# Moving work from GpSimd and the residual of one output group in a streaming mixer layer

## The chip, the cores and the metric

The kernel runs on one core of one Trainium2 chip. The metric is the device time of one execution in microseconds: the median of the runs shown. The profile is of one further execution of the same program.

Engines are named as in the profile: PE is TensorE's matmul, PEld its weight load, DVE is VectorE, ACT is ScalarE, POOL is GpSimd, SP is SyncE, which here only issues DMAs.

## The reference

One mixer layer is applied to 1024 rows of a new stream and 64 rows of a running one, with 2048 features each:

```
h = RMSNorm(x);  z = h @ w_in                      # 2048 x 7296, 57 blocks of 128 columns
A: vn = LayerNorm(gelu(v));  f = tril(W_s) @ vn + b   # per 128-row chunk and head group
   out_a = gelu(u) * f * silu(g_a)
B: zs mixed with its previous row (token shift) -> r, k, v, and two low-rank inputs
   decay = exp(-exp(-softplus(-d) - 0.5)), a = sigmoid(...)
   kk = k * k_k / |k * k_k|;  k = k * (1 + (a - 1) * k_a)
   S = S * decay - (S kk) (kk a)^T + v k^T;  y = S r     # 16 heads of 64, over time
   y = GroupNorm(y) + (sum r k r_k) v;  out_b = y * silu(g_b)
o = [out_a ; out_b] @ w_out;  y = RMSNorm(x + o)
```

Outputs are the normalised rows of both streams, the final states S, the last shifted rows and the vn of the running stream.

## The kernel before, in words

**Precision and tiling.** Large products are made of three float16 matmuls each (high and low halves of both operands, line list `PASSES`). The normalised input lies transposed in SBUF as two float16 copies in one large tile (`bigt`, 16 blocks of 1088 columns each). The input projection walks over 57 weight blocks; each block takes three groups of 364, 364 and 360 columns with 48 matmuls, into one of two PSUM banks called `mp`. A weight block is loaded as float32 (`raw`), scaled and split into its two halves by ACT and DVE (`w`).

**Pairs.** Part B treats the 16 heads as 8 pairs. The generator `front(q)` (line 825) prepares pair q: low-rank products, decay and its running products, the normalised kk, the new k, and whole-tile products of 128x1088 that end as the packed tiles AR and KB. The generator `wkv(q)` (line 928) takes chunks of 64 rows in groups of up to four: two matmuls per chunk and head fill a PSUM bank (`bigp`) with four 64x64 blocks per chunk (the Gram blocks). Those are copied to the tile MK (named `wk` in the profile, as AR, KB and others share it) and multiplied by a strictly lower or a lower triangular mask. A triangular inverse on DVE follows (60 small products and transposes), then a chain of 17 chunk steps in which PE makes a 128x128 product (`yps`), DVE adds it to the values, PE makes the next (`smp`), and DVE updates the state S. `post(q)` normalises, gates and writes the result to HBM.

**Output.** The output weights come in 16 jobs: two halves of the 16 feature blocks times 8 groups of 256 columns. `out_first` (line 1355) does group 0 of the first half; it does the first six feature blocks of four row blocks and then the last two, as these come late. Then `out_group` does the others. Each group's accumulator is a slice of `bigt` (`acc_view`), whose place is free once the input projection has read it. It is loaded with x, the residual, by `acc_load` (line 1410), and `out_add` (line 1348) adds a scaled PSUM bank to it on DVE. Loads for groups 1 to 7 go out on POOL's queue, that for group 0 on ACT's.

**Order.** The order on every engine is written out by a planner in Python at build time. It keeps a clock for each engine (`self.clk`), charges each instruction an estimated cost (`act`, `stt`, `tt`, `mm`), and walks through PE's main work, the projection. Between matmuls `poll()` lets side generators go on whose due time (the value they yielded) has come, and only if DVE's clock is not further ahead of PE's than the generator's backlog. A generator that waits for a flag or for room in PSUM yields until it is there. Engines run their instructions strictly in that order; only semaphores hold them up on the chip.

**Places that the change touches.** In the profile nearly all instructions stand under a helper's line: 186 is `act`, 194 `stt`, 203 and 201 `tt`, 245 `mm`, 253 `dma`. Line 201 is the branch of `tt` that cuts a whole-tile product on POOL into two instructions; the planner charges both together 200 ns and 2.2 ns a column. On DVE it charges 150 ns and one column per 0.96 GHz cycle.

Of the kernel before, what the change touches and what calls it, by code (L numbers as in the profile page):

```python
# [10 lines left out]
AF = mybir.ActivationFunctionType  # L11
ALU = mybir.AluOpType
# [4 lines left out]
NP, NS = 1024, 64  # L17
# [27 lines left out]
class Builder:  # L45
# [779 lines left out]
    def front(self, q):  # L825
        nc = self.nc
# [4 lines left out]
        for j in range(2):  # L831
            f = self.dma(nc.sync, lw[:, j], self.a["lora"][j, :, q * 128:(q + 1) * 128], 1 << 16)
# [3 lines left out]
        for j in range(2):  # L836
            f = self.act(self.lwh[:, j, 0], lw[:, j], AF.Copy, scale=self.lws[j][0])
        yield f - 200
        for j in range(2):
            f = self.stt(self.lwh[:, j, 1], lw[:, j], self.lws[j][0], self.lwh[:, j, 0], ALU.mult, ALU.subtract, dep=f)  # L840
        yield max(f, fh)
        c = yield from self.galloc(RES)
        C = self.U(c)
# [3 lines left out]
        f = self.fin(DV, 2800)  # L847
        fh = self.dma(nc.sync, hw, self.hw_d[:, NT:2 * NT], 1 << 18)
        yield f
        p = yield from self.galloc(RES)  # L850
        PX = self.u[p][:, 0:NCH * 65].rearrange("p (c t) -> p c t", t=65)
        nc.gpsimd.memset(PX[:, :, 0:1], 1.0)
        v3 = lambda x: x.rearrange("p (c t) -> p c t", t=64)
# [5 lines left out]
        aa = self.U(ai)  # L859
# [3 lines left out]
        k = yield from self.z_load(32 + q, RES)  # L863
        K = self.U(k)
        sq = yield from self.galloc(RES)
        SQ = self.U(sq)
        yield self.act(SQ, K, AF.Square, scale=self.vcol(V_KK, q))
        for hs in self.head_sums(SQ):
            if isinstance(hs, tuple):
                f = self.act(hs[0], hs[1], AF.Ln)  # L870
# [4 lines left out]
        yield self.stt(SQ, SQ, 1e12, K, ALU.min, ALU.mult)  # L875
        t = yield from self.galloc(RES)
        T = self.U(t)
        yield self.tt(T, SQ, aa, ALU.mult, eng=nc.gpsimd)
        yield self.ts(aa, aa, self.vcol(V_KA, q), self.oka[:, q:q + 1], ALU.mult, ALU.add)
        yield self.tt(K, K, aa, ALU.mult, eng=nc.gpsimd)  # L880
        self.free(ai)
        yield self.tt(T, T, C, ALU.mult, eng=nc.gpsimd)
        yield self.tt(v3(SQ), v3(SQ), PX[:, :, 0:64], ALU.mult, eng=nc.gpsimd)
        if q:
            yield from self.wait(("c16", q - 1))
        for hp in HP:
# [1 line left out]
        r = yield from self.z_load(24 + q, RES)  # L888
        R = self.U(r)
        RP = PX[:, :, 1:65]  # L890
        yield self.tt(RP, v3(R), RP, ALU.mult, eng=nc.gpsimd)
        yield self.stt(R, R, self.vcol(V_RK, q), K, ALU.mult, ALU.mult)
        yield self.tt(K, K, C, ALU.mult, eng=nc.gpsimd)
        self.free(c)
        yield from self.wait("f")
        v = P["v"] = yield from self.z_load(40 + q, RES)
        V = self.U(v)
        nk = self.nkk[:, q:q + 1]
        for part, (c0, c1) in enumerate(PARTS):
# [6 lines left out]
            f = self.copy(self.AR[:, cs, 1, :], RP[:, cs])  # L906
            for i in range(2):
                ci = slice(c0 + i, c1, 2)
                f = self.act(self.KB[:, ci, 1 - i, :], v3(T)[:, ci], AF.Copy, scale=nk)
                f = max(f, self.copy(self.KB[:, ci, i, :], v3(K)[:, ci]))  # L910
# [5 lines left out]
        for hs in self.head_sums(R, V):  # L916
            if isinstance(hs, tuple):
                f = self.tt(hs[2], hs[1], hs[2], ALU.mult)
# [4 lines left out]
        f = self.dma(nc.sync, self.bv_d[q], V, 1 << 19)  # L923
# [4 lines left out]
    def wkv(self, q):  # L928
        nc = self.nc
        P = self.pr[q]  # L930
        AR, KB, MK, KBt, VS = self.AR, self.KB, self.MK, self.KBt, self.VS
        v3 = self.U(P["v"]).rearrange("p (c t) -> p c t", t=64)
# [3 lines left out]
        mv = MK.rearrange("p (r c) g k -> p c r g k", r=2)  # L936
# [69 lines left out]
        for part, (c0, c1) in enumerate(PARTS):  # L1006
            yield from self.wait(("ark", q, part))
            self.add(vtr(part), backlog=1e9)
            for c in range(c0, c1, 4):
                m = min(4, c1 - c)  # L1010
                yield from self.room("big", "big")
                pts = [self.bigt() for _ in range(2)]
                for r in range(m):
                    for h in range(2):
                        self.mm(pts[h][:, r * 128:(r + 1) * 128], KB[HP[h], c + r].rearrange("p s t -> p (s t)"),
                                AR[HP[h], c + r].rearrange("p s t -> p (s t)"))
                for h in range(2):
                    f = self.act(mv[:, c:c + m, :, h, :],
                                 pts[h][:, 0:m * 128].rearrange("p (c r k) -> p c r k", r=2, k=64), AF.Copy)
                for r in range(2):  # L1020
                    v = MK[:, 17 * r + c:17 * r + c + m]
                    f2 = self.tt(v, v, self.mask[:, r * 64:r * 64 + 64].unsqueeze(1).unsqueeze(1)
                                 .to_broadcast([128, m, 2, 64]), ALU.mult, eng=nc.gpsimd, dep=f)
                    fm = fm if r else f2
                a0, a1 = max(c, 1), min(c + m, 16)
                if a0 < a1:
                    self.tt(af[:, a0:a1], af[:, a0:a1], pc[:, a0 - 1:a1 - 1].unsqueeze(2)
                            .to_broadcast([128, a1 - a0, 128]), ALU.mult, eng=nc.gpsimd)
                yield f - 300
            self.add(ktr(part), backlog=1e9)  # L1030
# [18 lines left out]
        for i in range(1, 31):  # L1049
            n = 31 - i  # L1050
# [3 lines left out]
            f = self.tt(X[:, i + 1:32, 0:i], X[:, i + 1:32, 0:i], pv, ALU.add)  # L1054
# [5 lines left out]
        f = self.vtr(ent(PT), X, rate=0.58)  # L1060
        yield f
        PG = PR.rearrange("p (c g t) -> p c g t", g=2, t=32)
        for p0, par, n in SIDE:
            self.act(MA[p0:p0 + 32, par:NCH:2, :, 0:32], PG[p0:p0 + 32, 0:n], AF.Copy)
            f = self.copy(MA[p0 + 32:p0 + 64, par:NCH:2, :, 32:64], PG[p0 + 32:p0 + 64, 0:n])
# [34 lines left out]
        pts = [self.bigt() for _ in range(2)]  # L1100
# [246 lines left out]

    def out_add(self, g, st, t, nt, ps):
        a = self.acc_view(g)[:, t:t + nt, :]
        while ("acc", g) not in self.flags:  # L1350
            self.spin()
        return self.stt(a, ps[:, 0:nt * 256].rearrange("p (t n) -> p t n", n=256), self.sc[st][:, 4:5], a,
                        ALU.mult, ALU.add)

    def out_first(self, st):
        w = self.wb[st]
        self.out_scale(0, st)
        self.add(self.acc_load())
        for t0 in (0, 4):
            ps = [self.ps_main.tile([128, 512], F32, tag="m", name="mp") for _ in range(2)]  # L1360
            for kts in (range(6), range(6, 8)):
                for p in range(2):
                    for r in range(2):
                        self.out_mm(0, ps[p], r, t0 + 2 * p + r, w, kts, kts[0] == 0 and r == 0, r == 1)
                    if kts[0]:
                        self.out_add(0, st, t0 + 2 * p, 2, ps[p])
        self.out_sample(0, w, self.mixT[0], self.sc[st][:, 4:5])

    def out_part(self, half, g, st, t, nt):
# [39 lines left out]

    def acc_load(self):  # L1410
        nc = self.nc
        self.accs = self.big[:, 16384:17408].rearrange("p (j t) -> p j t", t=64)
        for g in range(8):
            if g == 1:
                yield from self.wait(("mixT", 0))
            if g >= 4:
                yield from self.wait("moved")
            self.dma(nc.gpsimd if g else nc.scalar, self.acc_view(g),
                     self.a["x"][0:NP, g * 256:(g + 1) * 256].rearrange("(t p) n -> p t n", p=128))
            if g == 0:  # L1420
                nc.gpsimd.dma_start(self.accs, self.a["xts"])
            self.flags.add(("acc", g))
            yield self.now + 10000

    def fg_load(self):
        while len(self.ufree) < 5:
# [218 lines left out]
```

## Time and profile before

| | |
|---|---|
| median of 3 runs | 1983.4 us (1980.28 to 1984.43) |
| profiled execution | 1978.55 us, its span 1976.8 us, granted PE clock 0.996 |
| PE busy | 1920.4 us (97%) |
| DVE busy | 1152.3 us (58%) |
| ACT busy | 1027.6 us (52%) |
| POOL busy | 352.5 us (18%) |

The span begins with the first instruction and ends with the last; the execution's time is 1.75 us longer. Busy time is the union of an engine's instructions. PE's matmuls are pipelined, so the durations of single ones overlap and their mean says little; the time of a long row of them, divided by their number, is what one costs. The input projection ends at about 1584 us; the output projection follows, with the last pair's chain laid over its first two groups.

### The profile page before, as it was taken

Reading aid. Unit: us, or ns where it says so; the run is one execution under the profiler, and the core shown is the slowest. Engines: PE = TensorE matmul, PEld = TensorE weight load, DVE = VectorE, ACT = ScalarE, POOL = GpSimd, SP = SyncE. Lnnn points to the kernel's source line nnn. Section 1 sums busy time; section 2 is a strip of 40 time slices with the busy share of each in tenths; the row PEclk is TensorE's granted clock in tenths of the full one; section 3 lists DMA queues with packets and bytes.
Section 4 is the critical chain, followed back from the end, with each engine's and each line's share of the span. In section 5 each row is a group of like instructions: output and inputs, shape, how many; then the busy total and the mean of one; then the engine's idle time right before and its main releaser. Section 6 shows DMA issues by size and latency. Waiting matters only on the chain. (4 is left out here: it accounts for less than half of the span.)

```text
span 1976.8 us, 42947 instructions
## 1 busy us (share of the span) xinstructions
PE 1920.4 (97%) x18429; PEld 1391.8 (70%) x18429; DVE 1152.3 (58%) x2557; ACT 1027.6 (52%) x1862; POOL 352.5 (18%) x360
## 2 busy tenths in 40 slices
PE   6999999999999999999999999999999989999998
PEld 5966666666666666676676666666666678899997
DVE  6574684355565658449559446564753776533444
ACT  7632344467556554755664746646564542422433
POOL 2400000320410340150231042033014311000000
PEclk9999999999999999999999999999999999999999
DMA  6221124213122322313212321221232355312114
GB/s 239 87 76 43 46 80 148 111 54 106 67 81 69 112 87 72 113 57 114 87 72 69 124 101 48 103 99 65 72 112 79 131 174 181 145 62 99 56 44 140
DMA packets 51758, 188.98 MB, mean 96 GB/s; under 512 B 6832, under 2 KB 18624, under 8 KB 41904
## 3 DMA queue, kind: packets, MB, share of 16 engines
q1 hardware_dynamic: 41200, 153.99, 22.3%
q0 software_dynamic: 6880, 22.26, 3.2%
q10 hardware_dynamic: 3488, 9.99, 1.3%
q8 instruction: 145, 2.38, 0.5%
q14 instruction: 45, 0.37, 0.1%
HBM read 140.32 MB, written 45.93 MB: 94 GB/s over the span
## 5 line engine op out<-in xcount | busy, mean ns | idle before, releaser
L245 PE MATMUL mp<-bigt,w 128*128 128x364 f16 (+3 forms) x8496 | 1323.1, 310 | 4.7 <-issue 2.6
L245 PEld LDWEIGHTS <-w 128*128 128x128 f16 x9216 | 815.8, 98 | 410.4 <-issue 3.9
L194 DVE SCALAR_TENSOR_TENSOR w<-raw,sci,w 128x512 f16<-128x512 f32 x276 | 221.7, 827 | 158.6 <-ACT w L186 157.8
L245 PEld LDWEIGHTS <-wk 128*128 128x128 f16 x2304 | 209.6, 98 | 28.5 <-issue 5.2
L186 ACT ACTIVATE w<-raw,sci 128x512 f16<-128x512 f32 x276 | 185.7, 713 | 57.9 <-DVE sci L303 49.1
L245 PE MATMUL mp<-w,wk 128*128 128x256 f16 x1728 | 203.7, 273 | 5.1 <-DVE bigt L194 5.1
L201 POOL TENSOR_TENSOR u<-u,u 128x544 f32<-128x544 f32 (+1 forms) x112 | 156.5, 1424 | 256.5 <-DVE u L194 105.4
L186 ACT ACTIVATE w<-raw 128x2048 bf16<-128x2048 f32 (+1 forms) x70 | 131.8, 1883 | 82.8 <-PE mp L245 82.2
L186 ACT ACTIVATE wk<-bigp 128x512 f32<-128x512 f32 (+6 forms) x248 | 121.0, 512 | 84.9 <-PE bigp L245 55.5
L245 PE MATMUL mp<-w,u 128*128 128x256 f16 x1152 | 141.2, 273 | 0.0
L186 ACT ACTIVATE u<-mp,sc 128x364 f32<-128x364 f32 (+3 forms) x109 | 57.0, 523 | 153.4 <-PE mp L245 152.6
L186 ACT ACT_TABLE_LOAD x91 | 116.8, 1283 | 23.4 <-PE smp L245 7.1
L194 DVE SCALAR_TENSOR_TENSOR bigt<-mp,sc,bigt 128x512 f32<-128x512 f32 (+2 forms) x83 | 54.1, 652 | 127.9 <-PE mp L245 127.5
L186 ACT ACTIVATE u<-yps 64x128 f32<-64x128 f32 x120 | 32.7, 273 | 182.8 <-DVE wk L203 182.1
L245 PEld LDWEIGHTS <-u 128*128 128x128 f16 x1152 | 112.1, 98 | 13.5
L1131 DVE SCALAR_TENSOR_TENSOR S<-S,pc,smp 64x64 f32<-64x64 f32 x240 | 66.8, 278 | 75.3 <-PE smp L245 70.5
L203 POOL TENSOR_TENSOR wk<-wk,mask 128x512 f32<-128x512 f32 (+1 forms) x80 | 83.2, 1059 | 137.8 <-ACT wk L186 137.8
L186 ACT ACTIVATE u<-mp,zs 128x364 f32<-128x364 f32 (+1 forms) x75 | 42.1, 562 | 121.4 <-PE mp L245 121.0
L203 DVE TENSOR_TENSOR u<-u,u 128x108 f32<-128x108 f32 (+15 forms) x248 | 91.4, 368 | 8.3
L203 DVE TENSOR_TENSOR u<-bigp,u 128x512 f32<-128x512 f32 (+3 forms) x72 | 41.5, 579 | 87.4 <-PE smp L245 57.0
L194 DVE SCALAR_TENSOR_TENSOR u<-mp,zs,u 128x363 f32<-128x363 f32 (+1 forms) x100 | 49.5, 495 | 66.8 <-ACT sht L186 35.4
L223 DVE STREAM_TRANSPOSE wk<-u 32x256 f32<-32x256 f32 (+1 forms) x128 | 58.0, 453 | 45.4 <-ACT u L186 43.5
(182 smaller groups left out, 1883.4 us busy)
## 6 DMA issues: line engine op xcount, KB each, us to landing
raw<-w_in SPq DMA_DIRECT2D x54, 1024.0 KB, 5.0
raw<-w_out SPq DMA_DIRECT2D x14, 1024.0 KB, 5.0
z_d<-u SPq DMA_DIRECT2D x24, 544.0 KB, 3.3
u<-z_d SPq DMA_DIRECT2D x24, 544.0 KB, 5.8
mix_d<-u ACTq DMA_DIRECT2D x16, 544.0 KB, 3.0
o_y<-bigt SPq DMA_DIRECT2D x16, 512.0 KB, 4.1
u<-mix_d POOLq DMA_DIRECT2D x15, 544.0 KB, 7.4
wk<-x SPq DMA_DIRECT2D x7, 1024.0 KB, 7.6
```

Of the source, the lines that this page charges most:

```text
L186: self.nc.scalar.activation(out, in_, func, bias=bias, scale=scale, **kw)
L194: self.nc.vector.scalar_tensor_tensor(out, in0, s, in1, op0, op1)
L201: eng.tensor_tensor(out[:, c], a[:, c], b[:, c], op)
L203: (eng or self.nc.vector).tensor_tensor(out, a, b, op)
L223: self.nc.vector.transpose(out, a)
L245: self.nc.tensor.matmul(out, lhsT, rhs, start=start, stop=stop)
L1131: self.nc.vector.scalar_tensor_tensor(Sn[hp, hp], Sc[hp, hp], pc[hp, c - 1:c], pu[hp, hp], ALU.mult, ALU.add)
```

## The change

Three edits go together.

1. The first output group is evicted by ACT as a plain scaled copy into its accumulator. Its share of x is no longer loaded ahead; after the last pair has been written out, it is loaded in two halves on SP's queue into two temporary tiles and added by DVE. The second half's eviction of group 0 waits for a flag, `("res", 0)`, that is set then. The loads of the other groups are issued without the planner's pause behind the first.
2. The Gram blocks are no longer copied by ACT and then masked in place by POOL in two instructions; DVE multiplies the PSUM bank by the mask as it evicts it. The generator yields after each of the two.
3. Six whole-tile products of `front` move from POOL (two instructions each) to DVE (one each).

```diff
@@ front
-        yield self.tt(T, SQ, aa, ALU.mult, eng=nc.gpsimd)
+        yield self.tt(T, SQ, aa, ALU.mult)
...
-        yield self.tt(K, K, aa, ALU.mult, eng=nc.gpsimd)
+        yield self.tt(K, K, aa, ALU.mult)
...
-        yield self.tt(T, T, C, ALU.mult, eng=nc.gpsimd)
-        yield self.tt(v3(SQ), v3(SQ), PX[:, :, 0:64], ALU.mult, eng=nc.gpsimd)
+        yield self.tt(T, T, C, ALU.mult)
+        yield self.tt(v3(SQ), v3(SQ), PX[:, :, 0:64], ALU.mult)
...
-        yield self.tt(RP, v3(R), RP, ALU.mult, eng=nc.gpsimd)
+        yield self.tt(RP, v3(R), RP, ALU.mult)
...
-        yield self.tt(K, K, C, ALU.mult, eng=nc.gpsimd)
+        yield self.tt(K, K, C, ALU.mult)
@@ wkv
                 for h in range(2):
-                    f = self.act(mv[:, c:c + m, :, h, :],
-                                 pts[h][:, 0:m * 128].rearrange("p (c r k) -> p c r k", r=2, k=64), AF.Copy)
-                for r in range(2):
-                    v = MK[:, 17 * r + c:17 * r + c + m]
-                    f2 = self.tt(v, v, self.mask[:, r * 64:r * 64 + 64].unsqueeze(1).unsqueeze(1)
-                                 .to_broadcast([128, m, 2, 64]), ALU.mult, eng=nc.gpsimd, dep=f)
-                    fm = fm if r else f2
+                    f = self.tt(mv[:, c:c + m, :, h, :],
+                                pts[h][:, 0:m * 128].rearrange("p (c r k) -> p c r k", r=2, k=64),
+                                self.mask[:, 0:128].rearrange("p (r k) -> p r k", k=64).unsqueeze(1)
+                                .to_broadcast([128, m, 2, 64]), ALU.mult)
+                    fm = f + 300
+                    yield f - 400
@@ out_add
-        while ("acc", g) not in self.flags:
+        while ("acc" if g else "res", g) not in self.flags:
@@ out_first
-        self.add(self.acc_load())
+        self.accs = self.big[:, 16384:17408].rearrange("p (j t) -> p j t", t=64)
+        self.add(self.acc_load(), backlog=1e9)
...
-                        self.out_add(0, st, t0 + 2 * p, 2, ps[p])
+                        t = t0 + 2 * p
+                        self.act(self.acc_view(0)[:, t:t + 2, :].rearrange("p t n -> p (t n)"), ps[p][:], AF.Copy,
+                                 scale=self.sc[st][:, 4:5])
+        while ("acc", 0) not in self.flags:
+            self.spin()
@@ acc_load
-            self.dma(nc.gpsimd if g else nc.scalar, self.acc_view(g),
-                     self.a["x"][0:NP, g * 256:(g + 1) * 256].rearrange("(t p) n -> p t n", p=128))
-            if g == 0:
+            if g:
+                self.dma(nc.gpsimd, self.acc_view(g), self.x_cols(g))
+            else:
                 nc.gpsimd.dma_start(self.accs, self.a["xts"])
             self.flags.add(("acc", g))
-            yield self.now + 10000
+            yield self.now + 10000 * (g > 0)
+        yield from self.wait(("mix", 15))
+        for h in range(2):
+            i = yield from self.galloc(1)
+            x = self.u[i][:, 0:1024].rearrange("p (t n) -> p t n", n=256)
+            yield self.dma(nc.sync, x, self.x_cols(0)[:, 4 * h:4 * h + 4], 1 << 19)
+            a = self.acc_view(0)[:, 4 * h:4 * h + 4]
+            yield self.tt(a, a, x, ALU.add)
+            self.free(i)
+        self.flags.add(("res", 0))
```

`x_cols(g)` is the slice of x that belongs to group g.

## Rows read from the trace of the kernel before

**Rows 1.** The page: busy us, share of span, instructions of each engine.

```profile
PE 1920.4 (97%) x18429; PEld 1391.8 (70%) x18429; DVE 1152.3 (58%) x2557; ACT 1027.6 (52%) x1862; POOL 352.5 (18%) x360
```

**Rows 2.** Windows, nine stretches from 300 to 1576 us: total length, busy us by engine.

```profile
sum 1276.00, PE 1249.77 PEld 841.11 DVE 754.38 ACT 746.57 POOL 298.90; mean PE 138.86 PEld 93.46 DVE 83.82 ACT 82.95 POOL 33.21
```

**Rows 3.** Timeline of the first output group: start, duration, instruction, [idle before, releaser].

```profile
1590.72 4.09 PE L245 MATMUL mp<-w,u 128*128 128x256 f16 x36
1590.73 0.42 ACTq L253 DMA_DIRECT2D bigt<-x  x1
1591.35 1.93 ACT L186 ACTIVATE w<-raw,sci 128x512 f16<-128x512 f32 x3
1591.89 0.78 DVE L194 SCALAR_TENSOR_TENSOR u<-bigt,pwi,u 128x544 f16<-128x544 f32 x1
...
1599.11 0.71 DVE L194 SCALAR_TENSOR_TENSOR bigt<-mp,sc,bigt 128x512 f32<-128x512 f32 x1
...
1599.87 1.44 PE L245 MATMUL mp<-w,wk 128*128 128x256 f16 x6 [5.06 <-DVE bigt L194]
...
1601.75 0.63 ACT L186 ACTIVATE wk<-u 32x512 f32<-32x512 f32 x1 [8.46 <-DVE u L223]
```

**Rows 4.** PE's timeline, three rows that begin after an idle time.

```profile
504.13 0.49 PE L245 MATMUL smp<-wk 128*128 128x128 f32 x2 [2.18 <-DVE wk L203]
...
1139.34 0.46 PE L245 MATMUL smp<-wk 128*128 128x128 f32 x2 [2.21 <-DVE wk L203]
...
1470.26 0.49 PE L245 MATMUL smp<-wk 128*128 128x128 f32 x2 [0.38 <-DVE wk L203]
```

**Rows 5.** Timelines of POOL and DVE, in a chain's steps and after the last.

```profile
498.70 5.03 POOL L201 TENSOR_TENSOR u<-u,u 128x544 f32<-128x544 f32 x4
499.44 4.33 DVE L211 TENSOR_SCALAR gss<-gss 64x2 f32<-64x2 f32 x1
...
651.96 3.60 POOL L201 TENSOR_TENSOR u<-u,u 128x544 f32<-128x544 f32 x2
652.25 2.13 DVE L203 TENSOR_TENSOR u<-u,gst 128x1024 f32<-128x1024 f32 x1
...
1440.49 0.16 DVE L211 TENSOR_SCALAR gss<-gss 64x2 f32<-64x2 f32 x1
...
1670.89 1.22 DVE L203 TENSOR_TENSOR u<-u,gst 128x1024 f32<-128x1024 f32 x1
```

**Rows 6.** Groups by form: line, engine, operation, shapes, count, busy us, mean ns.

```profile
L201 POOL TENSOR_TENSOR u<-u,u 128x544 f32<-128x544 f32 x80 | 115.1, 1462 | 222.8 <-DVE u L194 105.4 <-issue 59.8 <-DVE u L213 45.2
L203 POOL TENSOR_TENSOR wk<-wk,mask 128x512 f32<-128x512 f32 x64 | 76.2, 1210 | 137.8 <-ACT wk L186 137.8
...
L201 POOL TENSOR_TENSOR u<-u,u 128x576 f32<-128x576 f32 x16 | 21.3, 1330 | 0.0
L201 POOL TENSOR_TENSOR u<-u,u 128x512 f32<-128x512 f32 x16 | 21.2, 1326 | 33.7 <-DMA u<-z_d 33.7
...
L203 DVE TENSOR_TENSOR u<-bigp,u 128x512 f32<-128x512 f32 x32 | 22.0, 690 | 81.7 <-PE smp L245 57.0 <-PE bigp L245 19.0 <-DMA f_d<-u 4.6
...
L203 DVE TENSOR_TENSOR u<-u,u 128x1088 f32<-128x1088 f32 x8 | 11.7, 1459 | 0.1
...
L203 POOL TENSOR_TENSOR wk<-wk,pc 128x512 f32<-128x512 f32 x24 | 26.8, 1117 | 0.0
...
L186 ACT ACTIVATE wk<-bigp 128x512 f32<-128x512 f32 x112 | 62.5, 595 | 67.2 <-PE bigp L245 43.6 <-PE bigp L250 22.5 <-PE smp L245 0.9
```

**Rows 7.** Timelines of ACT and PE: last pair's final pass, group 0's second half.

```profile
1690.54 1.11 ACT L186 ACTIVATE u<-u 128x1088 f32<-128x1088 f32 x1 [7.78 <-DVE u L194]
...
1788.97 4.09 PE L245 MATMUL mp<-w,wk 128*128 128x256 f16 x36
```

**Rows 8.** Windows, two neighbouring stretches: bounds, then length and busy us.

```profile
1150.00:1200.00 50.00, 48.32 (x387) 32.93 (x385) 16.75 (x42) 25.32 (x49) 26.74 (x25) 1.00 0.26 89
1200.00:1250.00 50.00, 50.00 (x446) 32.33 (x444) 44.95 (x103) 24.02 (x43) 3.46 (x5) 1.00 0.21 68
```

In these two rows the columns after the length are the busy times of PE, PEld, DVE, ACT and POOL with their instruction counts, then the granted PE clock, the DMA engines' share and GB/s.

More of the change, by code (lines that the diff above doesn't have):

```diff
@@ L1411, in acc_load @@
         nc = self.nc
-        self.accs = self.big[:, 16384:17408].rearrange("p (j t) -> p j t", t=64)
         for g in range(8):
@@ L1417, in acc_load, with x_cols @@
                 yield from self.wait("moved")
-            self.dma(nc.gpsimd if g else nc.scalar, self.acc_view(g),
-                     self.a["x"][0:NP, g * 256:(g + 1) * 256].rearrange("(t p) n -> p t n", p=128))
-            if g == 0:
+            if g:
+                self.dma(nc.gpsimd, self.acc_view(g), self.x_cols(g))
+            else:
                 nc.gpsimd.dma_start(self.accs, self.a["xts"])
             self.flags.add(("acc", g))
-            yield self.now + 10000
+            yield self.now + 10000 * (g > 0)
[8 more added lines that the diff above has]
+        self.flags.add(("res", 0))
+    def x_cols(self, g):
+        return self.a["x"][0:NP, g * 256:(g + 1) * 256].rearrange("(t p) n -> p t n", p=128)
     def fg_load(self):
```

## The prediction

> **What bounds the kernel now.** I read the busy times of the page first. TensorE (PE) is busy 1920.4 us of a span of 1976.8 us [rows 1], so a change that leaves every matmul as it is, as this one does, can only win back idle time of PE: 56.4 us in all. No more than that is at stake, whatever the other engines save. The start (PE idle while the first rows of x are normalised) and the tail after the last matmul are not touched. The stretch that the change does touch runs from 300 us, where the pairs begin, to the first output group at 1600 us. From 300 to 1576 us PE is busy 1249.77 of 1276.00 us, so 26.2 us are idle [rows 2], and one more gap of 5.06 us follows at 1599.87 us [rows 3].
>
> The next view is PE's timeline, of which I took the rows that carry an idle time in brackets. Two things are to be seen there [rows 4]. Most gaps stand in front of the small float32 matmuls of the state chain (tiles smp and yps) and name VectorE (DVE) as the releaser: DVE is late with the sum or the new state that the next step multiplies. Between 300 and 1576 us I count 23 gaps of 0.38 us or more, 25.1 us together. During 12 of them, the first at 504.13 and the last at 1470.26 us, GpSimd (POOL) was in one of its whole-tile products; these are 11.75 us. The other 11 sum to 13.4 us and have other causes: an early wait for a write to HBM, DVE held up behind a ScalarE (ACT) result (the 2.21 us at 1139.34), and stretches where PE waits for nothing that the profile shows.
>
> The timeline of DVE and POOL side by side says why POOL matters [rows 5]. A DVE TENSOR_SCALAR on 64x2 elements, 0.16 us when POOL is quiet (1440.49), starts at 499.44 and takes 4.33 us: it ends at 503.77, as POOL's row of 5.03 us that began at 498.70 ends at 503.73. The chain's addition stood behind it, and PE lost 2.18 us. In the same way a product of 128x1024 took 2.13 us at 652.25, under POOL's row of 3.60 us from 651.96, and 1.22 us at 1670.89, where POOL did no arithmetic.
>
> **The change part by part.** *First output group.* Today its eviction adds the residual, whose load was issued on ACT's queue at 1590.73 us; DVE evicts at 1599.11 (0.71 us), and PE, which needs the bank for its second four blocks, stands still for 5.06 us until 1599.87 [rows 3]. After the change ACT evicts with a scale and no load is needed. ACT is done with the weight preparation at 1591.35 + 1.93 = 1593.28 us and then waits until 1601.75. One eviction of 128x512 from PSUM costs ACT about 0.60 us [rows 6]. PE's first bank is complete twelve matmuls ahead of the second, 1.4 us at 4.09 us for 36, so it is free when PE comes back: the whole gap goes. What is late next is the eighth tile of the output's left operand, whose last piece DVE finishes at 1591.89 + 0.78 = 1592.67 us, about when PE gets to it. If DVE is a microsecond later there, PE stands for that microsecond. I bound the gain by 3 and 5.3 us and take 5.
>
> The residual of that group comes back at the end of the last pair: two loads on SP's queue, two DVE additions of 128x1024 at 1.22 us [rows 5]. The last pair's ACT pass ends at 1690.54 + 1.11 = 1691.65 us and the group's second half starts on PE at 1788.97 [rows 7]. SP's queue may hold the loads behind one weight load, which is paced by a group of 22 us; some 75 us are left. I cost this at nothing; if the cover were gone, PE would wait for a load, at most the 8.4 us from issue to use of the present one (1590.73 to 1599.11).
>
> In the same step the samples' load stays on POOL's queue and the loads for groups 1 to 7 may go out up to 10 us of planner time earlier, behind the same POOL waits as before: nothing.
>
> *Whole-tile products.* Of the 112 POOL half products [rows 6], 16 belong to the spatial-gating outputs and stay; 96 (48 whole tiles, six per pair) move. POOL loses 96/112 of 157.6 us, 135 us. DVE gains 48 times about 1.29 us (the 1.22 us of 128x1024 scaled to 1088 columns; the 1.46 us of the eight such products on DVE today holds stretched ones), 62 us.
>
> *Masks.* Per pair there are ten ACT copies out of PSUM (eight of 128x512, two of 128x128) and ten POOL products. All 80 copies go, 64 x 0.595 us and 16 short ones, some 43 us of ACT; POOL loses 76.2 us and the short ones [rows 6]. DVE gains 64 x 0.69 us and 16 short ones at about 0.3 us (an estimate from the 512-wide row), 49 us. The Trainium skill (VectorE: DVE Perf Modes, The TRN2 errata) gives a larger fixed cost to a VectorE read of PSUM than to one of SBUF, and a ScalarE read of PSUM as the cheaper one: an estimate by its formulas is 658 and 570 ns for 512 columns, so 64 evictions would lose 5.6 us of engine time. The rows give 690 and 595 ns, so 6.1 us; neither reaches the sum, because no wait of PE in [rows 4] is for these tiles.
>
> So DVE goes from 1152 to about 1152 + 111 us less what it no longer loses to stretching: near 1240 us, 63% of the span. Where does it land? In the stretch 1150 to 1200 us POOL is busy 26.74 and DVE 16.75 of 50 us; in 1200 to 1250 POOL 3.46 and DVE 44.95 [rows 8]. The moved work belongs to the stretches in which DVE has room; DVE's dense stretch (the triangular inverse) has next to none of it.
>
> *What PE gets.* Of the 11.75 us, POOL's remaining 16 half products of 112 keep 16/112, 1.7 us: 10 us are won. The least is 0 (the lateness stays, by another cause), the most all 26 us of the stretch, if the earlier and more regular DVE also mends the gaps that I put to other causes.
>
> *What the moved work costs.* It adds waits on DVE's own queue: an eviction is issued right behind its matmuls, so DVE can stand until PE has done them, and behind it stand the chain's state updates and the weights' low halves. PE waits for the former. The planner carries DVE's clock and sends the chain's next matmul only when that clock says ready, and its price for a product (150 ns and 1088/0.96, so 1.28 us) fits the 1.29 above, where its price for POOL (200 + 1088 x 2.2, so 2.59 us) is below the 2 x 1.46 us that the row shows. So I take a small cost. From below: none. From above: if half of the 48 products held up a chain step for their full length, 31 us. Today five gaps, 5.4 us, are DVE being late without POOL, over 754 us of DVE work in the same stretch [rows 2]; 111 us more at that rate are 0.8 us. I take 2.
>
> **Sum.** -5 - 10 + 2 = -13 us. Against the profiled execution (1978.55 us, span 1976.8) this is 1965.5 us; the median of the runs shown, 1983.4, lies 4.9 us above that execution, so the forecast for a median is 1970 us.
>
> **Rivals.** *A: more gaps close than I count.* For it: all the chain gaps share one form. Against it: 13.4 us have no POOL beside them. With 10 us more, 1960 us.
>
> *B: the lock stays.* POOL keeps 16 half products of 1.46 us and 32 scalings of the queries, and each of these may still stretch a DVE instruction that PE waits for. Against it: the products left are few and the scalings sit in the mask stage. If PE loses as much to these, the sum is -5 + 2 and the time 1980 us. The Trainium skill (SBUF — State Buffer, Who interferes with whom) says that VectorE and GpSimd share a pair of ports which whoever starts first holds for a whole instruction, and that a VectorE instruction with two SBUF inputs is among those that compete: by that rule the moved products become new victims of the POOL work left, and the masked evictions, with one input in PSUM, do not. The 4.33 us row agrees with the first half; no row here shows the second.
>
> *C: DVE becomes the late one (slower).* Place: the last part of a pair's chain, over which the next pair's products and first evictions are laid. Price: 1.29 us for a product and 1.4 us for two evictions in front of a state update. It decides once about a dozen of the 128 moved instructions each make PE wait a full length, since 12 x 1.29 cancels the 15 us won. With 24 of them, -15 + 31 gives 1999 us. Against it: the stretches above, and the planner's clock.
>
> *D: the first group gains nothing*, because the eighth tile or ACT is late there instead: -10 + 2, 1975 us.
>
> **Chances.** Forecast (1962 to 1976 us) 0.60; A 0.10; D 0.07; B 0.13; C 0.10. A measurement of this kernel tells about 0.2% from no change, 4 us, so faster means under 1979.4 and slower over 1987.4. B lies on the edge: half of it counts as the same, with 0.03 of C. Faster 0.83, same 0.10, slower 0.07. The range 1957 to 1982 us leaves out the far end of A and nearly all of C.
>
> **What would show it.** Right: PE's gap at the first output group gone; POOL near 135 us busy, DVE near 1240, ACT near 985; no DVE instruction of the 64x2 kind above 1 us in a chain; PE's idle time from 300 us to the end of the input projection down from 26 to about 18 us, with PE's busy time unchanged. Wrong: chain gaps as many as before with a DVE product or a masked eviction as the row in front (C) or a POOL row beside them (B); a gap in the first output group that names another releaser (D).

## The result, and the profile after

The changed kernel takes 1964.4 us (median of four runs, 1963.49 to 1966.56) against 1983.6 us before (1980.28 to 1984.43), a ratio of 0.9909 with a 95% interval of 0.9896 to 0.9922: 18 us faster by the ratio, 19 by the medians. The forecast was 1970 us, its range 1957 to 1982. The profiled execution takes 1964.30 us with a span of 1962.6 us, so between the two profiled executions the difference is 14.2 us, where the sum said 13. The other 4 to 5 us are no gain of a stretch: the earlier kernel's profiled execution is 4.9 us faster than its median, the later one's lies at its median.

Busy times of the engines, from the page of the kernel after:

```profile
PE 1917.9 (98%) x18429; PEld 1392.4 (71%) x18429; DVE 1224.0 (62%) x2683; ACT 994.0 (51%) x1787; POOL 134.8 (7%) x184
```

Against [rows 1], PE's idle time over the span fell from 56.4 to 1962.6 - 1917.9 = 44.7 us, with as many matmuls. That is 11.7 of the 14.2 us; the other 2.5 are PE's busy time. From 300 to 1576 us, the stretch of [rows 2], the sum row of the windows is now (busy us by engine):

```profile
sum 1276.00, PE 1257.60 PEld 847.63 DVE 845.12 ACT 715.97 POOL 81.90; mean PE 1257.60 PEld 847.63 DVE 845.12 ACT 715.97 POOL 81.90
```

So 18.4 us are idle there, against 26.2 us before. For the experiments I split the time into the loop over the pairs, 300 to 1500 us, and the transition from the input projection to the output, 1500 to 1700 us, which contains the first output group. PE's idle time is a row's length less its PE busy time. The kernel before (columns as in [rows 8]):

```profile
1500.00:1700.00 200.00, 191.73 (x2090) 150.09 (x2089) 125.67 (x266) 87.69 (x156) 42.10 (x50) 0.98 0.45 156
300.00:1500.00 1200.00, 1176.43 (x10971) 793.12 (x10969) 709.68 (x1656) 700.07 (x1231) 270.19 (x262) 1.00 0.26 89
```

and the kernel after:

```profile
300.00:1500.00 1200.00, 1183.80 (x11055) 798.89 (x11053) 789.20 (x1796) 676.53 (x1177) 72.82 (x105) 1.00 0.26 90
1500.00:1700.00 200.00, 195.64 (x2139) 156.59 (x2138) 132.54 (x278) 92.45 (x158) 23.36 (x35) 1.00 0.47 167
```

The loop idles 16.2 us instead of 23.6, the transition 4.4 instead of 8.3. The durations of the moved work, from the groups by form (columns as in [rows 6]):

```profile
L194 DVE SCALAR_TENSOR_TENSOR w<-raw,sci,w 128x512 f16<-128x512 f32 x276 | 203.3, 762 | 121.0 <-ACT w L186 120.1
L203 DVE TENSOR_TENSOR u<-u,u 128x1088 f32<-128x1088 f32 x56 | 72.1, 1292 | 3.7 <-DMA u<-z_d 3.1
...
L203 DVE TENSOR_TENSOR wk<-bigp,mask 128x512 f32<-128x512 f32 x64 | 42.9, 685 | 52.8 <-PE bigp L245 52.7
...
L211 DVE TENSOR_SCALAR gss<-gss 64x2 f32<-64x2 f32 x8 | 1.3, 163 | 0.3
```

A product takes 1.292 us (forecast 1.29), a masked eviction 0.685 us (0.69). The 64x2 instruction, 787 ns in the mean of its eight before and 4.33 us at worst [rows 5], now has a mean of 163 ns. The first row, the low half of a weight, is unchanged in the code; its mean was 827 ns. The two groups in the kernel before:

```profile
L194 DVE SCALAR_TENSOR_TENSOR w<-raw,sci,w 128x512 f16<-128x512 f32 x276 | 221.7, 827 | 158.6 <-ACT w L186 157.8
...
L211 DVE TENSOR_SCALAR gss<-gss 64x2 f32<-64x2 f32 x8 | 6.3, 787 | 0.3
```

### The profile page after: what moved, and what is told of

Read it like the earlier page. It is cut to its first block, busy times and chain, and to the rows that moved or that the text cites. A ratio compares the mean times of both kernels' runs of the same rounds, so it can differ in the third digit from the quotient of the medians.

```text
span 1962.6 us, 42787 instructions
## 1 busy us (share of the span) xinstructions
PE 1917.9 (98%) x18429; PEld 1392.4 (71%) x18429; DVE 1224.0 (62%) x2683; ACT 994.0 (51%) x1787; POOL 134.8 (7%) x184
## 4 chain that ended last, share of the span: by engine, by line
PE 88%; ACT 5%; DVE 4%; issue 1%; DMA 1%; SPq 0%; DVEq 0%; ACTq 0%
PE mp L245 76%; PE bigp L245 7%; PE smp L245 2%; ACT u L186 2%; PE bigp L250 1%; PE yps L245 1%; ACT wk L186 1%; ACT L186 1%; DVE w L194 1%; DVE u L194 1%; ACT w L186 1%; DVE u L203 1%; DVE wk L203 1%; PE bigp L947 0%; DMA f_d<-u 0%
## 5 line engine op out<-in xcount | busy, mean ns | idle before, releaser
L194 DVE SCALAR_TENSOR_TENSOR w<-raw,sci,w 128x512 f16<-128x512 f32 x276 | 203.3, 762 | 121.0 <-ACT w L186 120.1
L203 DVE TENSOR_TENSOR u<-u,u 128x1088 f32<-128x1088 f32 (+15 forms) x296 | 152.8, 517 | 12.0 <-DMA u<-z_d 3.1
L245 PE MATMUL mp<-w,u 128*128 128x256 f16 x1128 | 137.2, 273 | 0.1
L186 ACT ACTIVATE wk<-bigp 64x512 f32<-64x512 f32 (+5 forms) x168 | 82.9, 503 | 87.4 <-PE bigp L250 69.0
L203 DVE TENSOR_TENSOR u<-u 128x30 f32<-128x30 f32 (+14 forms) x240 | 79.9, 333 | 6.1
L203 DVE TENSOR_TENSOR wk<-bigp,mask 128x512 f32<-128x512 f32 (+1 forms) x80 | 46.9, 605 | 57.2 <-PE bigp L245 57.2
L245 PE MATMUL bigp<-wk 64*128 64x128 f32 (+3 forms) x1584 | 74.4, 246 | 0.2 <-DVE wk L203 0.2
```

The source lines that it names most:

```text
L186: self.nc.scalar.activation(out, in_, func, bias=bias, scale=scale, **kw)
L194: self.nc.vector.scalar_tensor_tensor(out, in0, s, in1, op0, op1)
L203: (eng or self.nc.vector).tensor_tensor(out, a, b, op)
L245: self.nc.tensor.matmul(out, lhsT, rhs, start=start, stop=stop)
```

## The experiments

The edits are numbered as in the section on the change. The theory: POOL's whole-tile products lengthen DVE's instructions beside them, and PE waits for those. Its rival: the order in which the planner lays the work changes with any edit, and that is what moves the gaps. "Loop" and "transition" are PE's idle us in the two stretches above. Each experiment has its own runs of the kernel before beside it (medians 1981.0 to 1983.6 us), and the ratio is to those. Idle times are of the one profiled execution of a kernel; it lies within 2.4 us of the median, except in the kernel before (4.9 us faster), the one before with the early load (5.3 us faster) and that with edits 1 and 2 (4.4 us slower).

| kernel | us | ratio, 95% | loop | transition |
|---|---|---|---|---|
| before | 1983.6 | | 23.6 | 8.3 |
| after (1, 2, 3) | 1964.4 | 0.9896 to 0.9922 | 16.2 | 4.4 |
| 1 alone | 1978.5 | 0.9976 to 0.9994 | 24.0 | 7.0 |
| 2 alone | 2009.8 | 1.0136 to 1.0163 | 28.6 | 25.8 |
| 3 alone | 1990.8 | 1.0037 to 1.0062 | 14.9 | 24.9 |
| 1 and 2 | 1991.6 | 1.0042 to 1.0068 | 28.7 | 12.4 |
| 1 and 3 | 1975.4 | 0.9958 to 0.9980 | 15.5 | 12.6 |
| 2 and 3 | 1981.8 | 0.9993 to 1.0012 | 16.0 | 15.7 |
| before, short POOL products | 1969.7 | 0.9932 to 0.9957 | 15.7 | 8.4 |
| 2 and 3, early load | 1965.0 | 0.9905 to 0.9934 | 16.3 | 5.4 |
| before, early load | 1977.4 | 0.9964 to 0.9982 | 23.2 | 5.4 |
| after, later drain | 1972.4 | 0.9938 to 0.9967 | 15.5 | 10.5 |
| after, priced wait | 1964.3 | 0.9899 to 0.9926 | 6.9 | 14.4 |
| after, gate product on DVE | 1976.1 | 0.9964 to 0.9984 | 14.0 | 11.6 |

The two columns leave out what the granted clock costs. PE's busy time over the span, for the same 18429 matmuls, is 1917.2 to 1921.3 us in the kernels whose granted clock in the transition is 0.97 or more, and 1920.2 to 1930.1 us in those with 0.91 (2 alone) to 0.96.

**Edit 1 alone.**

```diff
@@ out_first, out_add, acc_load: edit 1 as in the change
-                        self.out_add(0, st, t0 + 2 * p, 2, ps[p])
+                        self.act(self.acc_view(0)[:, t:t + 2, :]..., ps[p][:], AF.Copy, scale=self.sc[st][:, 4:5])
```

> Only the first output group's edit (scaled eviction by ACT, residual added late). Theory L (PE's lost time in the chain is VectorE being held up by GpSimd's whole-tile products; the first group's gap is a separate 5 us): 5 us less than before, about 1978.5 us, PE idle from 300 us to the end of the input projection unchanged near 26 us. Theory O (the gain comes from the new order that the planner writes, whatever edit disturbs it): any change of 3 to 15 us, with gaps in the chain at other places.

It gained 0.15%, 3 us. The gap of 5.06 us is gone, but three others stand in the last pair behind it, in PE's timeline of this kernel:

```profile
1616.88 0.46 PE L245 MATMUL bigp<-wk,u 64*64 64x64 f32 x16 [1.67 <-issue]
...
1620.14 0.16 PE L245 MATMUL smp<-sc,ones 128*128 128x1 bf16 x1 [1.21 <-ACT wk L186]
...
1635.28 0.46 PE L245 MATMUL yps<-S,wk 128*128 128x128 f32 x2 [0.94 <-DVE S L1131]
```

These are 3.8 us, so of 5 us won the transition keeps 1.3.

**Edit 2 alone.**

```diff
@@ wkv: edit 2 as in the change
-                    f = self.act(mv[...], pts[h][...], AF.Copy)
+                    f = self.tt(mv[...], pts[h][...], self.mask[...], ALU.mult)
```

> Only the masks, applied as VectorE evicts the Gram blocks. Theory L: GpSimd's masks stand beside few steps of the chain, so 0 to 2 us less, 1981 to 1984 us; the gaps beside whole-tile products stay. Theory R (ACT was the engine that made VectorE late, and the 43 us taken from ACT are what helped): 6 to 10 us less, about 1975 us.

It is 1.5% slower, and in both stretches (windows of this kernel):

```profile
300.00:1500.00 1200.00, 1171.43 (x10928) 789.16 (x10926) 745.60 (x1723) 671.42 (x1162) 196.15 (x192) 1.00 0.26 89
1500.00:1700.00 200.00, 174.25 (x1784) 132.07 (x1783) 119.06 (x260) 77.63 (x139) 28.39 (x37) 0.91 0.43 151
```

The loop loses 5.0 us: I had costed the masks at nothing. Its longest gap shows how they can lose there (POOL, DVE and PE):

```profile
714.52 5.16 DVE L219 COPY wk<-u 128x128 f32<-128x128 f32 x1
...
715.97 2.62 POOL L201 TENSOR_TENSOR u<-u,u 128x544 f32<-128x544 f32 x2
...
719.84 1.27 DVE L203 TENSOR_TENSOR wk<-bigp,mask 128x512 f32<-128x512 f32 x2
720.57 1.11 PE L250 MATMUL bigp<-ident,wk 128*128 128x128 f32 x4 [2.95 <-DVE wk L203]
```

A small DVE copy (0.21 us in the mean of its 24 before) takes 5.16 us while POOL is busy without a break from 714.96 to 719.59 us, with the gate product and two scalings, which all three edits leave there; the masked evictions stand behind the copy on DVE, and PE waits for them. Before, ACT took the blocks out of PSUM. In the transition one gap stands out; PE's timeline has

```profile
1637.61 1.01 PE L245 MATMUL mp<-w,wk 128*128 128x256 f16 x4 [15.57 <-DVE bigt L194]
```

the eviction of the first output group, with its residual, a wait three times as long as in [rows 3].

**Edit 3 alone.**

```diff
@@ front: edit 3 as in the change, six times
-        yield self.tt(K, K, C, ALU.mult, eng=nc.gpsimd)
+        yield self.tt(K, K, C, ALU.mult)
```

> Only the whole-tile products, on VectorE instead of GpSimd. Theory L: 10 us less for the gaps beside GpSimd, 1 to 2 us more for VectorE's added work, about 1975 us, and nearly all of the PE idle time saved lies in the chains. Theory R: 0 to 3 us, 1980 to 1983 us. Theory C (VectorE late by its added work): slower than before.

The loop gains 8.7 us, most of what the sum gave to the products, and the kernel is still 0.5% slower; the 1975 us expected of the theory missed, by the transition. PE, DVE and the queues in the transition (ACTq is ACT's queue of DMA issues):

```profile
1596.79 0.94 POOL L253 DMA_DIRECT2D bigt<-x  x1
...
1598.54 1.77 POOL L253 DMA_DIRECT2D bigt<-x  x2 [0.82 <-DVE bigt L194]
...
1599.83 0.42 ACTq L253 DMA_DIRECT2D bigt<-x  x1
...
1617.14 0.75 DVE L194 SCALAR_TENSOR_TENSOR bigt<-mp,sc,bigt 128x512 f32<-128x512 f32 x1 [13.64 <-DMA bigt<-x]
...
1617.94 1.01 PE L245 MATMUL mp<-w,wk 128*128 128x256 f16 x4 [13.22 <-DVE bigt L194]
```

The first group's residual was issued last, at 1599.83 us, behind three other groups' loads on POOL's queue, and DVE waited for it until 1617.14: 17.3 us from issue to use, where [rows 3] show 8.4.

**The same order with short products on POOL.** This takes POOL's time away without moving any instruction: the order on PE, DVE, ACT and SP is that of before. Six of the seven POOL whole-tile products of a pair (five in `front`, the one of the spatial gate) compute one column of each half (the two that are written by blocks of 64, one block); the other columns are left out of the computation.

```diff
@@ tt
-            for c in (slice(0, h), slice(h, out.shape[1])):
+            for c in ((slice(0, 1), slice(h, h + 1)) if one else (slice(0, h), slice(h, out.shape[1]))):
@@ front, and the gate product
-        yield self.tt(K, K, C, ALU.mult, eng=nc.gpsimd)
+        yield self.tt(K, K, C, ALU.mult, eng=nc.gpsimd, one=True)
```

> The kernel before with the same order of instructions on PE, DVE, ACT and SP; of GpSimd's seven whole-tile products of a pair all but the first are cut to one column each half (they are left out of the computation). Theory L: the waits beside GpSimd go without any new order, 9 to 12 us less, about 1973 us, and VectorE's mean for the weights' low halves falls from 827 to about 760 ns. Theory O: the order is the same, so the time stays within 3 us of 1983.

Sum over the loop, and the weights' low halves by form:

```profile
sum 1200.00, PE 1184.32 PEld 800.67 DVE 695.43 ACT 708.07 POOL 170.38; mean PE 1184.32 PEld 800.67 DVE 695.43 ACT 708.07 POOL 170.38
```

```profile
L194 DVE SCALAR_TENSOR_TENSOR w<-raw,sci,w 128x512 f16<-128x512 f32 x276 | 205.7, 769 | 164.2 <-ACT w L186 163.4
```

With nothing reordered, PE's idle time in the loop falls from 23.6 to 15.7 us, DVE's busy time by 14 us (over the whole span by 26.8 us, for the same 2557 instructions), and the mean low half from 827 to 769 ns. The time falls by 0.56%, 11 us. Of the 12 gaps that the prediction put down to POOL, 8 fall under 0.25 us (8.3 us), and 3 of the other 4 stand beside the product left at full length. All 11 that it put down to other causes are still there, 14.6 us against 13.4, such as the one of 1139.34 us [rows 4]:

```profile
1132.51 0.46 PE L245 MATMUL smp<-wk 128*128 128x128 f32 x2 [2.21 <-DVE wk L203]
```

A shorter product also gives its result earlier, but that is not what helped: in the kernel before, the waits for POOL's products in the loop are 0.6 us in all, on PE's weight loads. That is the theory shown for the loop. And since 15.7 us without the products is about the 16.2 us with them on DVE, the moved work costs about 0.5 us there, an estimate, as the two orders differ.

**Edits 2 and 3**, with the old residual.

```diff
@@ wkv, front: edits 2 and 3 as in the change; out_first, out_add, acc_load as before
```

> Masks and products on VectorE, the first output group as before. Theory I (the edits act on two places: in the loop the products win 8 us, and the new order makes the residual's load for the first group late, so the group's gap grows to 13 to 16 us as in the two kernels with one of these edits alone): 1983 to 1990 us, with a PE gap over 12 us in the first output group that names VectorE's eviction. Theory S (the edits add up: 29 us for the masks alone and 10 us for the products alone): about 2020 us.

No change in time (0.9993 to 1.0012), under the 1983 to 1990 us expected: the loop gains as in the whole change, the transition loses as much. The first group waits 9.05 us, not the 12 or more expected:

```profile
1609.65 1.03 PE L245 MATMUL mp<-w,wk 128*128 128x256 f16 x4 [9.05 <-DVE bigt L194]
```

Windows of 5 us around that wait (after the busy times: granted clock, DMA share, GB/s):

```profile
1595.00:1600.00 5.00, 3.88 (x17) 2.51 (x17) 3.30 (x9) 0.27 (x1) 0.00 (x0) 0.50 0.69 231
1600.00:1605.00 5.00, 0.60 (x3) 0.12 (x1) 0.00 (x0) 0.00 (x0) 0.00 (x0) 0.50 0.99 332
1605.00:1610.00 5.00, 0.35 (x2) 0.28 (x3) 1.13 (x3) 0.06 (x1) 0.00 (x0) 0.50 0.60 227
1610.00:1615.00 5.00, 5.00 (x26) 3.69 (x24) 1.99 (x6) 1.03 (x4) 0.00 (x0) 0.50 0.00 0
1615.00:1620.00 5.00, 5.00 (x45) 4.36 (x43) 3.18 (x10) 0.42 (x3) 0.00 (x0) 1.00 0.01 3
```

The DMA engines are 99% busy while PE stands, and PE then works at the lower clock level, 1.2 GHz, until about 1615 us, 5 us of it busy throughout, with 26 matmuls in these 5 us and 45 in the next. So this gap cost more than its length.

**Edits 1 and 3.**

```diff
@@ out_first, out_add, acc_load, front: edits 1 and 3 as in the change; wkv as before
```

> First output group and products, the masks left with ACT and GpSimd. Theory I: the loop's 8 us and the first group's 5 us both come, 1966 to 1970 us; the masks on VectorE are then worth 0 to 4 us. Rival (the masks are needed, since ACT and GpSimd are late with the last pair): 1975 us or more.

0.31% faster, where 1966 to 1970 us had been expected and the rival 1975 or more: the loop is as good as the whole change's, the transition loses 8.2 us to it. Two of its gaps:

```profile
1590.02 0.76 PE L245 MATMUL yps<-st,wk 128*128 128x128 f32 x2 [3.01 <-ACT wk L186]
...
1592.92 0.80 PE L245 MATMUL smp<-wk 128*128 128x128 f32 x2 [2.14 <-DVE wk L203]
```

They are state steps of the last pair, with no other matmul laid between. So the masks on DVE are worth 8 us of the transition's idle time beside the other two edits, though they alone cost 5 us in the loop. Their place alone does not remove these two gaps: with 2 alone they are 2.87 and 2.10 us, with 1 and 2 they are 3.19 and 2.10.

**Edits 2 and 3, residual loaded early.** The planner holds `acc_load` back while DVE's planned work runs ahead; edit 1 lifts that hold by one argument. Here that argument comes alone.

```diff
@@ out_first, on edits 2 and 3
-        self.add(self.acc_load())
+        self.add(self.acc_load(), backlog=1e9)
```

> As the kernel with masks and products, but the residual's load of the first group is issued without regard to VectorE's planned backlog. Theory I with the planner's backlog test as the cause of the late load: the first group's gap falls from over 12 us to 6 us or less and the time by 8 to 12 us. If the load is late for another cause (it waits for the place in SBUF, or stands behind three other loads of 1 MB), the gap stays over 10 us and the time within 3 us of the kernel without this edit.

1965.0 us, within the interval of the whole change. The load is issued at 1578.84 us, and the gap is

```profile
1593.97 0.81 PE L245 MATMUL mp<-w,wk 128*128 128x256 f16 x6 [2.50 <-DVE bigt L194]
```

Nothing has to be left out of the first group: the date of its load was the point, beside edits 2 and 3.

**Edits 1 and 2.**

```diff
@@ out_first, out_add, acc_load, wkv: edits 1 and 2 as in the change; front as before
```

> First output group and masks, the whole-tile products left with GpSimd. Theory I: the loop keeps its 28 us of PE idle time of the kernel with the masks alone (GpSimd's products still stretch VectorE, which now has the masked evictions too), and the 15.6 us gap of the first group goes: 1988 to 1994 us, slower than before. If the products are not what the loop's gain needs: loop idle under 20 us and about 1975 us.

0.55% slower. The loop is at 28.7 us as with 2 alone, so the masks' loss there is reproduced with another end of the program; in the transition the late load is gone.

**The early load on the kernel before.**

```diff
@@ out_first, on the kernel before
-        self.add(self.acc_load())
+        self.add(self.acc_load(), backlog=1e9)
```

> The kernel before with one argument changed: the residual's load of the first group is planned without regard to VectorE's backlog. If the late load is what makes PE's gap of 5 us there: the gap falls to 0 to 3 us and the time by 2 to 5 us, to about 1978 us, with the chains' gaps unchanged (24 us of idle time from 300 to 1500 us). If the eviction is late because VectorE is busy with the last pair's inverse: the gap stays at 5 us and the time at 1982.

0.27% faster: the load goes out at 1582.20 us and the gap of 5.06 us shrinks to 0.96 us, in a profiled execution of 1972.03 us against a median of 1977.4. By the medians this one argument does as much as edit 1 alone.

**A later drain of the token shift**, tried on the kernel after against its remaining gaps in the loop.

```diff
@@ in_group, on the kernel after: moved from before ps = self.ps_main.tile(...) to before inv = ...
+        if self.zmix is not None:
+            for _ in self.zmix:
+                pass
+            self.zmix = None
```

> The changed kernel with one edit more: the second step of the token shift (VectorE's additions that read ACT's copies) is no longer issued right at the start of the next column group but when the planner's due time has come, at the latest at that group's end. Theory A (the chain gaps left in the changed kernel, 0.9 to 2.8 us each at 790, 939, 959, 1096 and 1279 us, come from VectorE standing behind ACT's copies in these additions): 4 to 9 us less than the changed kernel, 1956 to 1960 us. If these gaps have another cause: within 3 us of 1964.

It failed: 8 us slower than after. The loop gains 0.7 us, the transition loses 6.1, with a wait of 4.17 us for ACT at 1576.80.

**The wait in the planner's books**, for the same gaps. In the kernel after the longest of them is (PE, ACT and DVE):

```profile
1275.97 1.28 ACT L186 ACT_TABLE_LOAD   x1
...
1277.88 0.56 ACT L186 ACTIVATE u<-mp,zs 128x364 f32<-128x364 f32 x1
...
1278.34 0.25 ACT L186 ACTIVATE zc<-mp,sc 128x1 f32<-128x1 f32 x1
...
1278.63 0.60 DVE L194 SCALAR_TENSOR_TENSOR u<-mp,zs,u 128x363 f32<-128x363 f32 x1 [3.56 <-ACT zc L186]
...
1279.26 0.28 DVE L203 TENSOR_TENSOR wk<-yps,wk 64x128 f32<-64x128 f32 x1
...
1279.59 0.49 PE L245 MATMUL smp<-wk 128*128 128x128 f32 x2 [2.75 <-DVE wk L203]
```

DVE stands 3.56 us for ACT's token-shift copy, which is behind a table load; the chain's addition is behind it on DVE, and PE waits for that. The planner's clock of DVE doesn't know of that wait; the edit tells it.

```diff
@@ z_mix, on the kernel after
-        f = self.stt(o[:, t0 + 1:t0 + m], ps[:, 0:m - 1], zs[:, 1:2], o[...], ALU.mult, ALU.add)
+        f = self.stt(o[:, t0 + 1:t0 + m], ps[:, 0:m - 1], zs[:, 1:2], o[...], ALU.mult, ALU.add, dep=f)
```

> The changed kernel, with the planner told that the token shift's first addition on VectorE can't start before ACT's copies are done (an argument that sets its due time; no instruction is added). Theory A (the gaps left in the chains are VectorE standing behind ACT's copies, unknown to the planner): idle time of PE from 300 to 1500 us falls from 16 to 8 to 11 us and the time to 1955 to 1960 us, if the end of the projection keeps its order. If the gaps have another cause, the loop's idle time stays at 15 to 17 us.

```profile
300.00:1500.00 1200.00, 1193.08 (x11101) 805.55 (x11100) 785.24 (x1772) 679.41 (x1171) 72.34 (x101) 1.00 0.26 91
1500.00:1700.00 200.00, 185.58 (x2080) 149.64 (x2079) 130.83 (x286) 81.77 (x147) 20.52 (x31) 0.97 0.43 151
```

The loop idles only 6.9 us, 9.3 less, and the transition 10.0 more, so the time is that of after. Of the new gaps, 6.5 us are four waits of output matmuls for their left operand (the longest 2.39 us at 1573.26, released by DVE's `bigt`); another of 2.56 us at 1621.58 is for an eviction. That loop with after's transition would be near 1964 - 10 = 1954 us, an estimate; no kernel with both was run.

**The gate product on DVE too**, the last whole-tile product on POOL.

```diff
@@ the gate product, on the kernel after
-        yield self.tt(self.U(gu), self.U(gu), self.U(f), ALU.mult, eng=nc.gpsimd)
+        yield self.tt(self.U(gu), self.U(gu), self.U(f), ALU.mult)
```

> The changed kernel, with GpSimd's last whole-tile product (gating, one per pair) on VectorE as well. Theory L: the 1 us gap at 1030 us beside it goes and VectorE's mean for the weights' low halves falls from 762 to about 748 ns; 1 to 3 us less in the loop, 1961 to 1964 us, if the end of the projection keeps its order; up to 10 us more if it does not.

The loop gains another 2.2 us and the low halves' mean falls to 752 ns, as the theory has it; the transition loses 7.2 us, PE's busy time is 5.5 us longer (1923.4 us, at a granted clock of 0.95 in the transition), and the kernel is 12 us slower than after. No version run beats the kernel after.

## Why the prediction was right, point by point

**The products: right, and shown.** The forecast gave PE 10 us in the stretch to 1576 us less 2 for the moved work; 7.8 us came. The short products show the cause, since they move nothing and close POOL's gaps alone. One reading of mine was too broad: POOL was in a whole-tile product during 9 of the 12 gaps (9.77 us); in the 3 others (695.20, 1003.25 and 1320.76 us) the product had ended 0.2 to 2.3 us before PE stood still, and they close with the short products too. A rule of the Trainium skill bears on it (SBUF — State Buffer, Who interferes with whom: VectorE and GpSimd share a pair of ports, whoever is first holds it for its instruction, and a VectorE instruction with two SBUF inputs is among those that compete for it). The low halves read two tiles in SBUF and lose 58 ns each in the mean with the short products, 16 us over 276; the runs agree with the rule but don't show the port itself. Two much stretched rows, the 64x2 instruction of 4.33 us and the copy of 5.16 us, read one tile each, so two inputs are not needed for it.

**The moved work: right in size.** 1.292 and 0.685 us a piece, about 0.5 us of PE's loop. POOL came to 134.8 us busy (135 forecast), DVE to 1224.0 (1240), ACT to 994.0 (985). Rival C, DVE as the late one, needed a dozen full-length waits and didn't come with edit 3.

**The masks: a term of nothing that held only in the loop and only beside the products.** I costed them at nothing because no wait of PE named their tiles. Alone they cost 5.0 us in the loop, twice (28.6 and 28.7 us); beside the products they cost nothing there (16.2 with, 15.5 without) and save 8 us in the transition. Neither is a matter of the eviction's price. What differs in the transition is the date of the operand's preparation. ACT's first conversions for the output begin, in the kernel after and in that with edits 1 and 3:

```profile
1523.28 2.65 ACT L186 ACTIVATE wk<-u,pwi 128x544 f16<-128x544 f32 x4
```

```profile
1538.84 0.74 ACT L186 ACTIVATE wk<-u,pwi 128x544 f16<-128x544 f32 x1
```

PE's first output matmul follows at 1579.98 and at 1571.30 us: a lead of 57 against 32 us. The kernel with edits 2 and 3 and the early load has a lead of 56 us and idles 5.4 us. But the kernel before with the early load has a lead of 29 us and idles 5.4 us as well, and those with 2 alone and with 1 and 2, whose masks are on DVE, have 34 us, so neither the lead alone nor the masks' place sets it. That is a reading of the rows; no run isolates it. In the loop, one gap of the masks alone is explained: the 2.95 us behind the stretched copy, 2.94 us in the kernel with 1 and 2. It is rival B's form of waiting, by work that POOL keeps in the whole change too; in the kernel after, that pair's gate product (703.23 us) has no gap of PE behind it. What brings the copy beside it in one order and not in the other, and the rest of the 5 us, stay open.

**The first output group: right in sign, for a cause that I saw only in part.** Forecast 5 us, measured 5.06 - 1.75 = 3.3 us. Rival D holds in small: ACT is late there, behind a table load and a weight conversion (ACT and PE, kernel after):

```profile
1591.52 1.28 ACT L186 ACT_TABLE_LOAD   x1
1592.82 0.32 ACT L186 ACTIVATE gst<-gst,eps 128x16 f32<-128x16 f32 x1
1593.04 0.70 ACT L186 ACTIVATE w<-raw,sci 128x512 f16<-128x512 f32 x1
1593.77 1.26 ACT L186 ACTIVATE bigt<-mp,sc 128x512 f32<-128x512 f32 x2
...
1594.51 0.82 PE L245 MATMUL mp<-w,wk 128*128 128x256 f16 x6 [1.75 <-ACT bigt L186]
```

What I did not see is that the old load's date hangs on DVE's planned work, which the other edits increase: without edit 1 the gap grew to 9.05 us. The effects don't add. Edits 1, 2 and 3 alone change the time by -0.15, +1.50 and +0.50%, which makes +1.9%, and together by -0.91%. Left out of the whole one at a time, edits 1, 2 and 3 are worth 18, 12 and 29 us by the ratios, where the sum had 5, 0 and 8. My sum over the parts came out for the whole because I priced the whole's stretches, not because each part was worth its term: that the transition fell into a good order with all three, 4.4 us of idle time where other combinations of the edits have 7.0 to 25.8, was luck, as I had no row for it. There the rival of the experiments, the planner's order, holds: the transition moves with every edit. PE's busy time, which I took as unchanged, gave 2.5 us, and the idle time 11.7 of the 13 forecast.

**The residual's return: right, free.** The load is issued at 1648.61 us and DVE's two additions follow, with no wait of PE for them:

```profile
1671.22 1.22 DVE L203 TENSOR_TENSOR bigt<-bigt,u 128x1024 f32<-128x1024 f32 x1
...
1675.83 1.22 DVE L203 TENSOR_TENSOR bigt<-bigt,u 128x1024 f32<-128x1024 f32 x1
```

**Rivals A and B.** A didn't come: 7.8 us is less than the 10 counted. The moved work is hardly stretched: a masked eviction takes 683 ns in the mean with all of POOL's products left (2 alone) and 685 here, a moved product 1.292 us here and 1.285 with the gate product gone from POOL too. B came in small, under POOL's remaining products (forecast 1.7 us kept):

```profile
1025.63 3.53 POOL L201 TENSOR_TENSOR u<-u,u 128x544 f32<-128x544 f32 x2
1026.75 2.96 DVE L194 SCALAR_TENSOR_TENSOR w<-raw,sci,w 128x512 f16<-128x512 f32 x2
...
1030.06 1.28 PE L245 MATMUL bigp<-u,bones 64*64 64x512 f32 x8 [0.96 <-DVE wk L203]
```

## What to carry to other kernels

Look for the instruction that is short when its neighbour engine rests and many times longer beside it: where such instructions feed the engine that bounds the kernel, moving the neighbour's work onto the engine that was slowed can pay, and shortening that work in an unchanged order is a test of it that moves nothing else. In a program whose order a planner writes, test edits together as well as one by one, and look at what each does to the issue date of loads that nobody touched. When a stretch improves and the total doesn't, compare the stretches by the bounding engine's idle time before doubting the improvement.

## What the runs showed that I had not expected

A load of 1 MB that takes 8.4 us from issue to use when it goes first took 17.3 us behind three others in the kernel with edit 3 alone, with a DMA share of 0.93 to 1.05 in the windows of 5 us from 1595 to 1615 us. After the wait in the kernel with edits 2 and 3 the granted clock stayed at 0.50 while PE was already busy again, and rose at about 1615 us. In the kernel before, the transition's mean granted clock is 0.98; in the kernel after, 1.00, and PE's busy time over the span is 2.5 us less for the same matmuls.
